# Low parts of the input projections' weights: a subtraction on VectorE, or a transfer that adds the weight to minus its high part

## The chip, the cores and the metric

The kernel runs on one core of a Trainium2 chip (trn2). The metric is the device time of one execution in microseconds (µs), as a median over runs. Five engines matter here, each with a queue of its own that it works through in order: PE (TensorE, matmuls), DVE (VectorE), ACT (ScalarE), POOL (GpSimd) and SP (SyncE, which here only issues DMA transfers). ACT and POOL issue transfers too. All transfers run on the core's 16 DMA engines.

## The reference

One decoder block on 512 tokens with 16 learned tokens ahead of them, 528 positions of width 1024:

```
h   = LN([meta; x])
p   = h @ W_in                      # 1024 -> 2048 (conformer) + 3360 (RWKV-7) + 2048 (two gates)
A   = proj(swish(LN(dwconv31(GLU(p_conv)))))
Bm  = proj(groupnorm(RWKV-7 recurrence over p_rwkv) * g)
h   = LN(alpha*h + (sigmoid(gA)*A + sigmoid(gB)*Bm) @ W_o)
out = LN(alpha*h + down(silu(u2)*u1)),   u = dwconv3(h @ ffn_up)
```

Everything is float32. The change concerns only how `W_in` is made ready for the matmuls of `p`.

## The kernel before, in words

**Two halves of each operand.** A matmul in the faster type float32r reads fewer bits than float32. So each operand is kept as a high part, rounded to float32r, and a low part, the rest. `gemm` (line 158) then adds up three products for each of the 8 slices of 128 input channels: high weight by high input (line 161), low weight by high input (162), high weight by low input (163). A weight tile of 128 output channels by 1024 input channels is 512 KB. It meets 528 columns in two halves of 272 and 256 (gates: 258 and 256), so one tile is worth 2 x 24 matmuls.

**Weights.** `wload` (line 155) and `wsplit` (143) make a tile ready: SP loads it into `wr` (two buffers), ACT rounds it into `wh` (line 138, in the helper `split`), DVE subtracts `wh` from `wr` into `wl` (line 141). `wh` and `wl` have two buffers each, so tile i can be written only once the matmuls of tile i-2 have read that buffer. There are 151 such tiles in the program. 59 are of `W_in`: 3 for the low-rank columns, and 56 in three functions: `rkv` (line 339, keys, values and receptances of a pair of heads, 24 tiles), `glu` (679, two tiles for each of 8 channel blocks, 16 tiles) and `gate` (730, 16 tiles).

**Order of the work.** `SCHEDULE` (line 47) lists the steps. For each of 8 pairs of heads: K is `rkv`; P is `prep` (decays, keys and the small products `Gt`); S is `solve` (a triangular system in 31 dependent steps on DVE, lines 521 and 523, with the taps of a depthwise convolution, lines 715 and 723, put between them); C is `merge` and `chain` (9 chunks of the recurrence, small matmuls at line 581); F is `finish`. G is `glu`, A is `gate`, N is the convolution's layer norm. The framework's scheduler then lays the instructions of each engine in one fixed queue by priority and its own estimate of when they can run. On PE the matmuls of the weight tiles stand between the small ones of `prep` and `chain`.

**POOL** has little work: memsets, a few small subtractions, and in each solve four small transfers for the first chunk of 16 positions: `dA` out (line 496), two of `L` in (507), `dT` out (539) and `Gt` in (556). The first of the 31 steps stand behind the arrival of `L` (line 527 reads it).

Of the kernel before, what the change touches and what calls it, by code (L numbers as in the profile page):

```python
# [11 lines left out]
F32 = mybir.dt.float32  # L12
F32R = mybir.dt.float32r
AF = mybir.ActivationFunctionType
ALU = mybir.AluOpType
# [3 lines left out]
P = 128  # L19
D = 1024  # L20
NK = D // P
# [17 lines left out]
C_GA = C_LORA + 288  # L39
# [15 lines left out]
def hybrid_block(ctx: ExitStack, tc: tile.TileContext, a, out, dbg=None):  # L55
    nc = tc.nc
    V, S, G, TE = nc.vector, nc.scalar, nc.gpsimd, nc.tensor
# [13 lines left out]
    def behind(ins, first, why):  # L71
        tc.add_manual_dep(ins.ins, first.ins.name, mybir.DependencyInfo(mybir.DependencyClass.NoSync,
                                                                mybir.DependencyReason.DATA), reason=why)
# [62 lines left out]
    def split(dst_hi, dst_lo, src, hi_engine="s"):  # L136
        if hi_engine == "s":
            S.copy(out=dst_hi, in_=src)  # L138
        else:
            V.tensor_copy(out=dst_hi, in_=src)  # L140
        V.tensor_tensor(out=dst_lo, in0=src, in1=dst_hi.bitcast(F32), op=ALU.subtract)  # L141

    def wsplit(raw_ap, shape, wpool, after=None, bufs=2):
        wpool = wpool or wp
        with nullcontext() if after is not None else front():
            raw = wp.tile(shape, F32, name="wr", tag="wr", bufs=2)
            load = nc.sync.dma_start(out=raw, in_=raw_ap)
            if after is not None:
                behind(load, after, "weights behind the input")
            hi = wpool.tile(shape, F32R, name="wh", tag="wh", bufs=bufs)  # L150
            lo = wpool.tile(shape, F32R, name="wl", tag="wl", bufs=bufs)
            split(hi, lo, raw)
        return hi, lo

    def wload(dram, c0, wpool=None, after=None, bufs=2):
        return wsplit(dram[:, c0:c0 + P].rearrange("(k p) n -> p k n", p=P), [P, NK, P], wpool, after, bufs)

    def gemm(ps, w, xh, xl, sl, nk=NK):
        wh, wl = w
# [8 lines left out]
    w_in = a["w_in"][0]  # L168
# [6 lines left out]
    def dcol(c, j=0, n=1):  # L175
        return drv[:, c + j:c + j + n]
# [28 lines left out]
    def shifted_gemm(dst, off, w, mi, rows=P):  # L205
        for hf in range(2):
            shifted_half(dst, off, w, mi, hf, rows)
# [15 lines left out]
    with tc.tile_pool(name="start", bufs=1, side="right", reuse_waits="tile") as st:  # L223
        prow = [st.tile([P, P], F32, name=f"prow{i}") for i in range(6)]
        with front():
            xt = []
            for i in range(5):
                n = NMETA if i == 0 else P
# [69 lines left out]
        c0 = 43  # L298
        for i, n in ((1, 112), (2, 128), (3, 120), (4, 88), (5, 44)):
# [15 lines left out]
                    in1=taps[:, :, 1, :], op=ALU.add)  # L315
# [23 lines left out]
    def rkv(p):  # L339
        k = ra.tile([P, OFF + T], F32, name="k", bufs=2)  # L340
        v = ra.tile([P, 64 + OFF + T], F32, name="v", bufs=2)
        r = ra.tile([P, OFF + T], F32, name="r", bufs=2)
        for i, (dst, c, off) in enumerate(((k, C_K, OFF), (v, C_V, OFF + 64), (r, C_R, OFF))):
            shifted_gemm(dst, off, wload(w_in, c + P * p), p + (8, 16, 0)[i])
        return r, k, v

    def prep(p, r, k, v):
# [329 lines left out]
    pair = lambda x: x.rearrange("p (m two) -> p two m", two=2)  # L677

    def glu(j):
        w2 = wload(w_in, 1024 + P * j)  # L680
        w1 = wload(w_in, P * j)
        cpad = ra.tile([P, 2, (KC - 1 + T) // 2], F32, name="cpad", bufs=3)
        G.memset(cpad[:, :, 0:KC // 2], 0.0)
        col2 = lambda t: (KC - 1 + t) // 2
        for t0, t1 in HALF:
            n = t1 - t0
            pt = gbank()
            gemm(pt[:, :n], w2, hh, hl, slice(t0, t1))
            with front():
                S.activation(out=cpad[:, :, col2(t0):col2(t1)], in_=pair(pt[:, :n]), func=AF.Tanh, scale=0.5)  # L690
        for t0, t1 in HALF:
            n = t1 - t0
            pt = gbank()
            gemm(pt[:, :n], w1, hh, hl, slice(t0, t1))
            with front():
                c_ = cpad[:, :, col2(t0):col2(t1)]
                V.scalar_tensor_tensor(out=c_, in0=c_, scalar=1.0, in1=pair(pt[:, :n]), op0=ALU.add, op1=ALU.mult)
        return cpad
# [28 lines left out]


    def gate(j):
        w = wload(w_in, C_GA + P * j)  # L730
        gt = sp.tile([P, NQ], F32, name="gt", bufs=2)
        for t0, t1 in QH:
            pt = gbank()
            n = t1 - t0
            gemm(pt[:, :n], w, hh, hl, slice(t0, t1))
            with front():
                S.activation(out=gt[:, t0 - Q0:t1 - Q0], in_=pt[:, :n], func=AF.Tanh, scale=0.5,
                             bias=dcol(D_HBG, j))
        nc.sync.dma_start(out=g_dr[j], in_=gt)
# [45 lines left out]
    raw, prs, solved, ys, cpads = {}, {}, {}, {}, {}  # L785
    gates = list(range(16))
    for step in SCHEDULE.split():
        what, p, q = step[0], int(step[1:2] or 0), int(step[2:] or -1)
# [23 lines left out]
    for j in range(NK):  # L812
        ga = rb.tile([P, NQ], F32, name="ga", bufs=2)
        nc.sync.dma_start(out=ga, in_=g_dr[j])
        w = wload(a["w_conv_out"][0], P * j)
# [12 lines left out]
    op = pool(ctx_o, "rout", "left")  # L828
# [10 lines left out]
    for j in range(NK):  # L839
# [4 lines left out]
        w = wload(a["w_rwkv_out"][0], P * j)  # L844
# [20 lines left out]
    for (t0, t1), (sl, n) in zip(QH, qsl):  # L865
# [3 lines left out]
        for j in range(NK):  # L869
            w = kept[j] if j < NKEEP else wload(a["w_o"][0], P * j)  # L870
# [3 lines left out]
            with front():  # L874
                V.scalar_tensor_tensor(out=x1, in0=hlo[:, j, t0:t1].bitcast(F32), scalar=ALPHA,
                                       in1=pt[:, :n], op0=ALU.mult, op1=ALU.add)
                V.scalar_tensor_tensor(out=x1, in0=hhi[:, j, t0:t1].bitcast(F32), scalar=ALPHA,
                                       in1=x1, op0=ALU.mult, op1=ALU.add)
# [57 lines left out]
    for j in range(2, NF):  # L936
        c = j - 2
# [80 lines left out]
```

## Time and profile before

| | |
|---|---|
| median of 3 runs | 1212.67 µs (1209.79 to 1213.87) |
| the profiled execution | 1205.18 µs, its span 1203.4 µs |
| PE busy | 1126.6 µs (94%) |
| DVE busy | 895.8 µs (74%) |
| ACT busy | 536.9 µs (45%) |
| POOL busy | 104.8 µs (9%) |
| moved by DMA | 119.00 MB |

A busy time is the union of an engine's instruction spans. Matmuls overlap, so a row of PE lasts longer (290 ns) than the distance to the next one (about 120 ns), and a busy PE need not be one at its peak. "Idle before, releaser" says how long an engine stood still ahead of an instruction and what ended that. The chain of waits is followed back from the last instruction to whatever released each piece of work.

### The profile page before, as it was taken

What the parts mean: (1) busy time and instruction counts of PE and PEld (TensorE: products, weight loads), DVE (VectorE), ACT (ScalarE), POOL (GpSimd) and SP (SyncE); (2) the same over time, 40 slices, a digit from 0 to 9 for tenths busy, and PEclk for the clock granted to TensorE, in tenths of its full rate; (3) what the DMA queues carried; (4) which work ended last, traced back from release to release, by engine and by line L of the source; (5) the groups of instructions that cost most, each with busy time, mean ns of one, the idle gap of its engine ahead of it and who ended that gap; (6) DMA issues with size and microseconds to landing.
All of it is one profiled execution on the core that took longest, in us unless ns stands there. A gap on an engine that the chain in (4) does not pass through costs nothing.

```text
span 1203.4 us, 22828 instructions
## 1 busy us (share of the span) xinstructions
PE 1126.6 (94%) x8718; PEld 1052.9 (87%) x8718; DVE 895.8 (74%) x2299; ACT 536.9 (45%) x1123; POOL 104.8 (9%) x250
## 2 busy tenths in 40 slices
PE   5999989899999979999886999999999999999997
PEld 3998979888898979999775989999999999998885
DVE  8599978988899898997487446688867666662227
ACT  3543445546455456565466333346443344431111
POOL 6001011201202021120200000000000000000000
PEclk9999999998999999999997999999999999999999
DMA  5233332333324233353541385622423233243221
GB/s 159 80 92 90 85 88 63 80 72 88 78 74 99 52 75 82 93 129 88 142 132 24 117 242 159 175 80 63 132 71 106 80 96 101 78 125 119 88 88 70
DMA packets 202440, 119.00 MB, mean 99 GB/s; under 512 B 50036, under 2 KB 186397, under 8 KB 202331
## 3 DMA queue, kind: packets, MB, share of 16 engines
q1 hardware_dynamic: 182992, 113.81, 33.4%
q10 hardware_dynamic: 17515, 3.17, 1.5%
q8 instruction: 68, 1.11, 0.4%
q0 software_dynamic: 1824, 0.57, 0.2%
q14 instruction: 41, 0.34, 0.1%
HBM read 102.24 MB, written 15.28 MB: 98 GB/s over the span
## 4 chain that ended last, share of the span: by engine, by line
PE 67%; DVE 18%; DMA 7%; issue 4%; ACT 4%; ACTq 0%; POOL 0%; DVEq 0%; SPq 0%; POOLq 0%
PE ps_g L161 16%; PE ps_g L163 15%; PE ps_g L162 15%; PE ps_x L581 8%; PE psf L962 3%; PE psf L964 3%; PE psf L963 3%; DVE wl L141 2%; DVE csh L715 2%; DVE cev L723 1%; DMA o_t<-o_dr 1%; DVE W L523 1%; DVE stmp L521 1%; DMA L<-dA 1%; DMA dA<-Gt 1%
## 5 line engine op out<-in xcount | busy, mean ns | idle before, releaser
L161 PE MATMUL ps_g<-hhi,wh 128*128 128x256 f32 (+2 forms) x1648 | 477.9, 290 | 14.0 <-ACT cpad L690 4.0
L163 PE MATMUL ps_g<-hlo,wh 128*128 128x256 f32 (+2 forms) x1648 | 475.6, 289 | 0.0
L162 PE MATMUL ps_g<-hhi,wl 128*128 128x256 f32 (+2 forms) x1648 | 475.5, 289 | 0.0
L161 PEld LDWEIGHTS ps_g<-hhi,wh 128*128 128x128 f32 x1648 | 313.0, 190 | 18.4 <-ACT hf_t L277 4.6
L163 PEld LDWEIGHTS ps_g<-hlo,wh 128*128 128x128 f32 x1648 | 313.0, 190 | 1.3
L162 PEld LDWEIGHTS ps_g<-hhi,wl 128*128 128x128 f32 x1648 | 312.2, 189 | 1.4 <-issue 0.4
L141 DVE TENSOR_TENSOR wl<-wr,wh 128x1024 fp32r<-128x1024 f32 x151 | 184.2, 1221 | 99.7 <-ACT wh L138 99.2
L138 ACT CAST wh<-wr 128x1024 fp32r<-128x1024 f32 x151 | 158.0, 1047 | 150.1 <-PE psf L963 75.2
L723 DVE SCALAR_TENSOR_TENSOR cev<-cd,drv,cev 128x257 f32<-128x257 f32 x216 | 98.2, 478 | 0.1
L920 ACT COPY pu<-ps_g 128x258 f32<-128x258 f32 (+1 forms) x88 | 32.9, 374 | 110.3 <-PE ps_g L163 110.2
L962 PE MATMUL psf<-wh,hidh 128*128 128x512 f32 x176 | 69.3, 394 | 0.0
L964 PE MATMUL psf<-wl,hidh 128*128 128x512 f32 x176 | 68.9, 391 | 0.0
L963 PE MATMUL psf<-wh,hidl 128*128 128x512 f32 x176 | 68.5, 389 | 0.0
L927 DVE SCALAR_TENSOR_TENSOR u<-pu,prm,u 128x512 f32<-128x512 f32 x88 | 65.7, 748 | 1.3
L581 PE MATMUL ps_x<-UV,Gt 128*66 128x64 f32 x576 | 59.2, 224 | 3.6 <-DMA Gt<-dT 1.7
L581 PEld LDWEIGHTS ps_x<-UV,Gt 128*66 128x66 f32 x576 | 53.5, 140 | 5.5 <-DVE on L673 2.3
L715 DVE SCALAR_TENSOR_TENSOR csh<-cpad,drv,csh 128x257 f32<-128x257 f32 x120 | 57.5, 479 | 0.4
L614 DVE SCALAR_TENSOR_TENSOR Sb<-Sb,lc,ps_x 64x64 f32<-64x64 f32 x112 | 31.3, 279 | 34.7 <-PE ps_x L581 33.1
L521 DVE TENSOR_TENSOR stmp<-L,W 128x60 f32<-128x60 f32 (+24 forms) x248 | 55.3, 223 | 1.1
L600 ACT COPY Rz<-ps_x 64x128 f32<-64x128 f32 x72 | 18.6, 259 | 82.6 <-PE ps_x L581 63.2
L523 DVE TENSOR_TENSOR W<-W,stmp 128x60 f32<-128x60 f32 (+24 forms) x248 | 53.3, 215 | 1.3
L925 DVE TENSOR_SCALAR u<-pu,prm 128x512 f32<-128x512 f32 x44 | 21.2, 484 | 43.1 <-ACT pu L920 43.0
(310 smaller groups left out, 2022.9 us busy)
## 6 DMA issues: line engine op xcount, KB each, us to landing
wr<-in_w_in_dram SPq DMA_DIRECT2D x59, 512.0 KB, 4.1
wr<-in_ffn_up_dram SPq DMA_DIRECT2D x44, 512.0 KB, 3.9
wr<-in_ffn_down_dram SPq DMA_DIRECT2D x22, 512.0 KB, 3.7
wr<-in_w_o_dram SPq DMA_DIRECT2D x10, 512.0 KB, 4.3
g_dr<-gt SPq DMA_DIRECT2D x16, 257.0 KB, 3.1
L<-dA SPq DMA_DIRECT2D x32, 128.0 KB, 3.8
wr<-in_w_conv_out_dram SPq DMA_DIRECT2D x8, 512.0 KB, 4.3
wr<-in_w_rwkv_out_dram SPq DMA_DIRECT2D x8, 512.0 KB, 5.3
```

The source lines that it names most:

```text
L138: S.copy(out=dst_hi, in_=src)
L141: V.tensor_tensor(out=dst_lo, in0=src, in1=dst_hi.bitcast(F32), op=ALU.subtract)
L161: TE.matmul(ps, wh[:, k, :], xh(k, sl), start=(k == 0), stop=False)
L162: TE.matmul(ps, wl[:, k, :], xh(k, sl), start=False, stop=False)
L163: TE.matmul(ps, wh[:, k, :], xl(k, sl), start=False, stop=(k == nk - 1))
L521: yield V.tensor_tensor(out=tv, in0=L[:, s, s + 1:32].unsqueeze(1).broadcast_to([P, nj, m]), in1=W[:, 0:nj, s:s + 1].broadcast_to([P, nj, ...
L581: mm = lambda o, l, r, start: TE.matmul(o, l, r, start=start, stop=True, skip_group_check=True)
L715: yield V.scalar_tensor_tensor(out=cs_, in0=x1[:, i:i + NM], scalar=dcol(D_SCW, 8 * i + j) if i < HT else dcol(D_HCW, 8 * 2 * i + j), in1= ...
L723: yield V.scalar_tensor_tensor(out=yp[:, b, :] if lasttap else ev[:, b, :], in0=d[:, i:i + NM], scalar=dcol(D_HCW, 8 * (2 * i + b) + j), i ...
L962: TE.matmul(acc[t][d], hidh[:, k, ts], wd[k][0][:, ds], start=(k == 0), stop=False)
L963: TE.matmul(acc[t][d], hidl[:, k, ts], wd[k][0][:, ds], start=False, stop=False)
L964: TE.matmul(acc[t][d], hidh[:, k, ts], wd[k][1][:, ds], start=False, stop=(k == NF - 1))
```

## The change

The functions that load weights get a parameter `add`, which `rkv`, `glu` and `gate` set. ACT still rounds the tile into `wh`. With `add`, ACT also writes minus the tile, rounded in the same way, into `wl`; then POOL issues a transfer that reads the 512 KB of the weight from DRAM a second time and adds it to what stands in `wl`. Without `add` the subtraction on DVE stays (95 tiles).

```diff
-    def wsplit(raw_ap, shape, wpool, after=None, bufs=2):
+
+    def wsplit(raw_ap, shape, wpool, after=None, bufs=2, add=False):
         wpool = wpool or wp
         with nullcontext() if after is not None else front():
             raw = wp.tile(shape, F32, name="wr", tag="wr", bufs=2)
             load = nc.sync.dma_start(out=raw, in_=raw_ap)
+            hi = wpool.tile(shape, F32R, name="wh", tag="wh", bufs=bufs)
+            lo = wpool.tile(shape, F32R, name="wl", tag="wl", bufs=bufs)
             if after is not None:
                 behind(load, after, "weights behind the input")
-            hi = wpool.tile(shape, F32R, name="wh", tag="wh", bufs=bufs)
-            lo = wpool.tile(shape, F32R, name="wl", tag="wl", bufs=bufs)
-            split(hi, lo, raw)
+            S.copy(out=hi, in_=raw)
+            if add:
+                S.mul(out=lo, in_=raw, mul=-1.0)
+                G.dma_start(out=lo, in_=raw_ap, accum_op=ALU.add)
+            else:
+                V.tensor_tensor(out=lo, in0=raw, in1=hi.bitcast(F32), op=ALU.subtract)
         return hi, lo
...
-            shifted_gemm(dst, off, wload(w_in, c + P * p), p + (8, 16, 0)[i])
+            shifted_gemm(dst, off, wload(w_in, c + P * p, add=True), p + (8, 16, 0)[i])
...
-        w2 = wload(w_in, 1024 + P * j)
-        w1 = wload(w_in, P * j)
+        w2 = wload(w_in, 1024 + P * j, add=True)
+        w1 = wload(w_in, P * j, add=True)
...
-        w = wload(w_in, C_GA + P * j)
+        w = wload(w_in, C_GA + P * j, add=True)
```

Lines behind this place carry numbers that are 6 higher after the change. The scheduler lays all queues anew.

The first place is ACT's queue at the three `W_in` tiles that are made ready while the first pair's `k`, `v` and `r` are projected (`k`, `v`, `r`: the projections that ACT and DVE take out of the PSUM bank `ps_g`, in halves of 272 and 255 columns). Before:

```order
L199 ACTIVATE k<-ps_g,prm 128x272
L199 ACTIVATE k<-ps_g,prm 128x255
L138 CAST wh<-wr 128x1024
L402 ACTIVATE sq<-k,prm 128x576
L199 ACTIVATE v<-ps_g,prm 128x272
L199 ACTIVATE v<-ps_g,prm 128x255
L138 CAST wh<-wr 128x1024
L199 ACTIVATE r<-ps_g,prm 128x272
L199 ACTIVATE r<-ps_g,prm 128x255
L138 CAST wh<-wr 128x1024
```

After:

```order
L205 ACTIVATE k<-ps_g,prm 128x272
L155 ACTIVATE wl<-wr 128x1024
L205 ACTIVATE k<-ps_g,prm 128x255
L153 CAST wh<-wr 128x1024
L408 ACTIVATE sq<-k,prm 128x576
L205 ACTIVATE v<-ps_g,prm 128x272
L155 ACTIVATE wl<-wr 128x1024
L205 ACTIVATE v<-ps_g,prm 128x255
L153 CAST wh<-wr 128x1024
L205 ACTIVATE r<-ps_g,prm 128x272
L155 ACTIVATE wl<-wr 128x1024
L205 ACTIVATE r<-ps_g,prm 128x255
```

The negation stands ahead of the second half of each projection, and the cast behind it.

The second place is POOL's queue around the second pair's solve (`dA`, `L`, `dT`: the small transfers of the solve). Before:

```order
L193 MEMSET r 128x49
L496 DMA dA_2233<-Gt 16x2x16
L507 DMA L_2245<-dA_2233 16x256 x2
L511 MEMSET W 128x256
L514 MEMSET W 32x8 x4
L458 TENSOR_TENSOR AR<-AR,lc 128x1024
L193 MEMSET v 128x113
L683 MEMSET cpad 128x2x15
L539 DMA dT_2235<-W_2246 32x16
L556 DMA Gt<-dT_2235 16x2x16
L515 COPY W_3280<-w_init 32x16
```

After:

```order
L156 DMA wl<-in_w_in_dram 128x8x128
L502 DMA dA_2248<-Gt 16x2x16
L513 DMA L_2260<-dA_2248 16x256 x2
L464 TENSOR_TENSOR AR<-AR,lc 128x1024
L156 DMA wl<-in_w_in_dram 128x8x128
L545 DMA dT_2250<-W_2261 32x16
L517 MEMSET W 128x256
L520 MEMSET W 32x8 x4
L199 MEMSET v 128x113
L562 DMA Gt<-dT_2250 16x2x16
L521 COPY W_3303<-w_init 32x16
L156 DMA wl<-in_w_in_dram 128x8x128 x3
```

An adding transfer now stands directly ahead of `dA` and one directly ahead of `dT`.

## Rows read from the trace of the kernel before

**Rows 1.** Busy time, share of the span, instructions; then stretch 50 to 600, DMA share last

```profile
PE 1126.6 (94%) x8718; PEld 1052.9 (87%) x8718; DVE 895.8 (74%) x2299; ACT 536.9 (45%) x1123; POOL 104.8 (9%) x250
50.00:600.00 550.00, 521.40 (x4294) 485.00 (x4294) 478.81 (x1519) 278.94 (x662) 81.51 (x173) 0.99 0.35 88
```

**Rows 2.** What PE waited for, 50 to 620: us in total, times, longest

```profile
PE ps_g L161 <- ACT cpad L690: 4.0, 1, 4.0
PE ps_g L161 <- DVE r L201: 3.7, 4, 1.4
PE ps_m L563 <- DVE t11n L558: 3.1, 2, 2.5
...
PE ps_x L581 <- DMA Gt<-dT: 1.7, 1, 1.7
PE ps_a L471 <- DVE Gt L453: 1.6, 2, 0.8
PE ps_x L581 <- DVE on L673: 1.5, 2, 1.1
PE ps_a L467 <- DVE Gt L453: 1.3, 1, 1.3
```

**Rows 3.** Chain of waits, 50 to 650, by line

```profile
by line: PE ps_x L581 13.6%; PE ps_g L161 11.5%; PE ps_g L163 11.0%; PE ps_g L162 10.9%; issue 6.2%; DVE wl L141 3.3%; DVE csh L715 3.0%; DVE cev L723 2.7%; DVE W L523 2.6%; DVE stmp L521 2.5%; DMA L<-dA 2.2%; DMA dA<-Gt 1.4%; DVE Gt L453 1
```

**Rows 4.** Costliest groups of the page: busy us, mean ns of one, idle before

```profile
L141 DVE TENSOR_TENSOR wl<-wr,wh 128x1024 fp32r<-128x1024 f32 x151 | 184.2, 1221 | 99.7 <-ACT wh L138 99.2
L138 ACT CAST wh<-wr 128x1024 fp32r<-128x1024 f32 x151 | 158.0, 1047 | 150.1 <-PE psf L963 75.2
```

**Rows 5.** DMA queue and issues, 50 to 600: KB each, us from issue to landing

```profile
q1 hardware_dynamic: 90073, 45.23, 31.4%
...
wr<-in_w_in_dram SPq DMA_DIRECT2D x52, 512.0 KB, 4.1
...
L<-dA POOLq DMA_DIRECT2D x16, 16.0 KB, 2.3
dA<-Gt POOLq DMA_DIRECT2D x8, 2.0 KB, 2.0
```

**Rows 6.** Timeline of POOL, 12 to 14: start, duration of transfers of 16 and 128 rows

```profile
12.82 0.52 POOL L243 DMA_DIRECT2D prow<-in_b_gate_dram  x1
13.33 0.58 POOL L245 DMA_DIRECT2D prow<-in_conv_dw_dram  x1
```

**Rows 7.** Timeline of PE, ACT, DVE at one tile of `glu`: start, duration

```profile
51.69 0.28 PE L163 MATMUL ps_g<-hlo,wh 128*128 128x256 f32 x1
...
52.00 0.39 ACT L690 ACTIVATE cpad<-ps_g 128x256 f32<-128x256 f32 x1 [1.85 <-PE ps_g L163]
52.28 1.04 ACT L138 CAST wh<-wr 128x1024 fp32r<-128x1024 f32 x1
...
53.36 1.23 DVE L141 TENSOR_TENSOR wl<-wr,wh 128x1024 fp32r<-128x1024 f32 x1 [3.55 <-ACT wh L138]
...
57.66 0.29 PE L161 MATMUL ps_g<-hhi,wh 128*128 128x272 f32 x1
```

**Rows 8.** Timeline of PE at the last of the 56 tiles: start, duration

```profile
603.58 0.36 PE L163 MATMUL ps_g<-hlo,wh 128*128 128x256 f32 x1
...
615.16 0.28 PE L161 MATMUL ps_g<-hhi,wh 128*128 128x258 f32 x1
```

**Rows 9.** Chain of waits at the second solve, 160 to 180: start, us, what

```profile
160.84 3.63 DMA dA<-Gt
...
165.04 0.44 POOL L L507
...
165.56 4.30 DMA L<-dA
169.88 0.22 DVE W L527
```

More of the change, by code (lines that the diff above doesn't have):

```diff
@@ L147, in wsplit, with wload @@
             load = nc.sync.dma_start(out=raw, in_=raw_ap)
+            hi = wpool.tile(shape, F32R, name="wh", tag="wh", bufs=bufs)
+            lo = wpool.tile(shape, F32R, name="wl", tag="wl", bufs=bufs)
             if after is not None:
                 behind(load, after, "weights behind the input")
-            hi = wpool.tile(shape, F32R, name="wh", tag="wh", bufs=bufs)
-            lo = wpool.tile(shape, F32R, name="wl", tag="wl", bufs=bufs)
-            split(hi, lo, raw)
+            S.copy(out=hi, in_=raw)
[4 more added lines that the diff above has]
+                V.tensor_tensor(out=lo, in0=raw, in1=hi.bitcast(F32), op=ALU.subtract)
         return hi, lo
-    def wload(dram, c0, wpool=None, after=None, bufs=2):
-        return wsplit(dram[:, c0:c0 + P].rearrange("(k p) n -> p k n", p=P), [P, NK, P], wpool, after, bufs)
+    def wload(dram, c0, wpool=None, after=None, bufs=2, add=False):
+        return wsplit(dram[:, c0:c0 + P].rearrange("(k p) n -> p k n", p=P), [P, NK, P], wpool, after, bufs, add)
     def gemm(ps, w, xh, xl, sl, nk=NK):
```

## The prediction, made before the changed kernel was run

> **What bounds the kernel now.** I read the busy times first. Over the span PE is busy 94%, and in the stretch from 50 to 600, in which nearly all of the 56 tiles are used, 521 of 550 µs, with DVE close behind at 479 (87%), ACT at 279 and POOL at 82 [rows 1]. So the question is whether DVE's 87% holds PE up. The list of PE's waits answers it: PE's visible waits on DVE in that stretch are few. The ones shown are 3.7 (a projection's evacuation), 3.1 (the merge), 1.6 and 1.3 (the small products) and 1.5 µs (`finish`) [rows 2], 11.2 µs together. The chain of waits says how far DVE stands behind PE where PE's own rows don't show it: the low-part subtraction, line 141, holds 3.3% of the chain from 50 to 650 [rows 3], 20 µs of 600. PE's own rows hold most of the chain. So this is a PE-bound stretch with DVE near the bound, and what DVE gets back is worth some 10 to 20 µs, not its whole busy time.
>
> **What goes.** 56 of 151 subtractions at 1.221 µs [rows 4] leave DVE, 68.4 µs of busy time. On the path they are worth between 0 (the next piece of DVE work, a tap of the convolution, takes the place) and 20 µs (all that the chain shows). I take 14: the 11.2 µs of waits shown and a little for those too short to be shown.
>
> **What comes, on ACT.** 56 negations of 128x1024. Nothing of that operation is in the trace; the nearest row is the cast of the same tile on the same engine, 1.047 µs [rows 4]. 56 x 1.047 = 59 µs, on an engine that is idle half of the stretch [rows 1]. As busy time I cost it at nothing. Its place costs something: in ACT's new queue the negation stands ahead of the second half of a projection's evacuation, which comes 1.05 µs later, and `r` of each pair feeds `prep`. Between 0 and 8 pairs x 1.05 = 8 µs; I take 3, since PE has other tiles to work on. Should PE have none left, it is the 8.
>
> **What comes, on POOL.** 56 transfers of 1024 runs of 512 bytes. POOL takes 0.52 µs to issue 16 rows and 0.58 for 128 [rows 6], 0.5 ns a row; 1024 rows would take about 1.0 µs by that line, an estimate. 56 µs on an engine that is busy 82 of 550 [rows 1]: hidden. Not hidden is the order. The queue is in order, the adding transfer waits for ACT, ACT's negation waits for PE to release the buffer, and now `dA` and `L` of a solve stand behind it. That pair of hops is on the chain already in the second solve: `dA` 3.63 µs, `L` 4.30 µs, then the first step of line 527 [rows 9]. The same small transfers land in 2.0 and 2.3 µs as a median [rows 5], so there was something ahead of them there. Behind an adding transfer each hop can lose its 2 µs of data: 0 to 8 pairs x 2 hops x 2 µs = 32 µs. I take 4, for a quarter of the hops and half of the 2 µs, because the second copy of the system, which comes through SP, has to arrive too.
>
> **The main term: when is `wl` ready.** Before, a tile whose buffer came free at 51.94 (0.25 µs after the start of the last matmul) had its cast at 52.28 and its subtraction done at 54.59, 2.7 µs after release; its first matmul came at 57.66 [rows 7]. So PE never waited for a low part there. I call the time from the last matmul of tile i-2 to the first of tile i the window: 57.66 - 51.94 = 5.7 µs here, 11.3 µs at the last of the 56 [rows 7, 8]. I measured all 56 in the same way: nine are 5.7 to 5.8 µs, ten lie from 6.1 to 7.7, and 37 from 8.7 to 20.4. After the change the window must hold the negation (1.05), the hand-over between engines (about 0.15) and the transfer from issue to landing, L.
>
> L is not in the trace. Bounds from the nearest rows: the plain load of the same 512 KB lands in 4.1 µs [rows 5]. Its packets took 31.4% of 16 engines over 550 µs for 90073 packets [rows 5], 30.7 ns each; 1024 packets on 16 engines are 2.0 µs of streaming, and the other 2.1 µs are latency, as the 2 KB transfer's 2.0 µs also say. An addition has to fetch what stands in `wl` as well. If that fetch costs nothing, L = 4.1; if it streams once more, L = 2.1 + 2 x 2.0 = 6.1; if reading back, adding and writing follow one another as two whole transfers, L = 8.2. I take 6.2, the middle, and keep both ends.
>
> Then I go through the 56 windows in order. A tile waits if 1.2 + L is longer than its window, and the wait lengthens the next window by as much, so in a run of short ones only every second pays. With L = 4.1 (5.3 µs) no window is too short. With L = 6.2 (7.4 µs) 12 tiles wait, **15 µs** together. With L = 8.2 (9.4 µs) 17 tiles wait, **41 µs**. The windows are those of the old PE queue; the new one breaks up some of the dense runs and makes others.
>
> The Trainium skill has a rule against this change. Its page "Collectives: The Full Stack", section "The bandwidth ceiling: the fold count and why AG ≠ RS ≠ AR", says that an addition inside a transfer is slow not for its arithmetic but because it needs two source reads, which halves the rate. No run here shows it yet. By it L would be the 6.1 and the sum mine; by the plain load's row the 15 µs would be nothing and the sum about 7 µs faster than before.
>
> **Sum.** -14 (DVE) + 15 (PE waits for `wl`) + 3 (evacuation) + 4 (solve's small transfers) = +8 µs on the profiled execution's 1205.18, which is 7.5 below the median of 1212.67. I carry the difference over to the median: **1221 µs**. A measurement of this kernel tells about 0.3% (3.6 µs) from no change.
>
> **Rivals.**
> 1. *Faster: the transfer lands like a plain load.* With L below about 4.5 no window is too short, and the whole of DVE's relief shows. For it: POOL's small transfers land in 2.0 µs, which is just the latency of the plain load [rows 5], and 37 of 56 windows have 3 µs to spare even at L = 4.3. Against it: the destination has to be read. Price: -20 (the subtraction's part of the chain [rows 3], with the costs of order hidden behind DVE's gain), so 1193. The skill's page "DMA: Bandwidth & Descriptors", section "Anatomy of one DMA — SWDGE (gpsimd) path", has a fit for transfers issued from GpSimd, 2.0 µs plus bytes over 436 KB per µs. For 512 KB that gives an estimate of 3.2 µs, under the 4.1 that this trace shows for a load through SP; it would put the time here.
> 2. *Much slower: the addition is slow or POOL's issue is.* With L = 8.2 the waits are 41 µs: -14 + 41 + 3 + 4 = +34, 1247; every further µs of L costs some 16 µs (17 to 24 tiles wait, most of them for all of it), so L = 9.5 gives about 1268. For it: a read and a write of the same bytes in one transfer, 1024 short runs, a conversion to float32r. Against it: POOL's issue time hardly grows with the rows [rows 6].
> 3. *It does nothing that can be seen:* DVE's relief is taken by the next tap, the windows of the new queue are long enough, 1213. The new queues show 56 transfers and 95 subtractions, so the change does say what it does.
>
> **Chances.** The forecast 0.44 (of that faster 0.06, same 0.11, slower 0.27; its own range 1208 to 1236), rival 1 0.33 (faster 0.29, same 0.04), rival 2 0.20 (slower), rival 3 0.03 (faster 0.01, same 0.01, slower 0.01). Together faster 0.36, same 0.16, slower 0.48. The range goes from 1184, rival 1 with another 9 µs from stalls too short for the list, to 1268, rival 2 at L = 9.5; what is left out is a slower addition still, or solves that lose the full 32 µs, and a larger gain.
>
> **What would show it.** Right: DVE 68 µs less busy, ACT 59 more, the adding transfer landing in 5.5 to 7 µs, and new waits of PE on it at line 168 (low weight) of some 15 µs, in 10 to 15 places, with the waits on DVE mostly gone. Wrong to the fast side: landing under 4.5 µs and no such waits. Wrong to the slow side: landing over 8 µs, or POOL busy for several µs at each issue, or long waits of line 527 for `L`. If the transfer lands as I say and the time still falls, my 14 µs for DVE was too little: then PE's hidden stalls between rows depend on DVE more than its waits show.

## The result, and the profile after

1278.96 µs as a median (1276.71 to 1287.9), against 1211.23 µs (1206.77 to 1213.87) of the kernel before on the same chip: slower by 5.8%, ratio 1.0577, 95% interval 1.0516 to 1.0638. That is 58 µs above the forecast and 11 µs above the upper end of the range. The profiled execution took 1278.51 µs, its span 1276.8.

The page of the changed kernel, busy times, granted clock, queues, groups and transfers:

```profile
PE 1153.7 (90%) x8718; PEld 1081.0 (85%) x8718; DVE 843.4 (66%) x2243; ACT 588.6 (46%) x1179; POOL 190.9 (15%) x306
...
PEclk9889899999998899999887799999999999999999
...
q0 software_dynamic: 60064, 29.93, 19.0%
...
L168 PE MATMUL ps_g<-hhi,wl 128*128 128x256 f32 (+2 forms) x1648 | 491.2, 298 | 68.1 <-DMA wl<-in_w_in_dram 68.1
...
L158 DVE TENSOR_TENSOR wl<-wr,wh 128x1024 fp32r<-128x1024 f32 x95 | 115.9, 1222 | 86.4 <-ACT wh L153 86.2
L156 POOL DMA_DIRECT2D wl<-in_w_in_dram x56 | 88.4, 1579 | 261.4 <-ACT wl L155 171.1
...
L155 ACT ACTIVATE wl<-wr 128x1024 fp32r<-128x1024 f32 x56 | 59.3, 1058 | 45.5 <-PE ps_g L168 40.1
...
wr<-in_w_in_dram SPq DMA_DIRECT2D x59, 512.0 KB, 5.2
wl<-in_w_in_dram POOLq DMA_DIRECT2D x56, 512.0 KB, 8.7
```

The 56 subtractions are gone: 95 of 151 are left, and their group falls from 184.2 µs [rows 4] to 115.9. DVE's busy time falls by 52 µs only [rows 1], since it is a union of spans and these overlap. The negation costs ACT 1.058 µs each, and the adding transfer lands in 8.7 µs. Issuing it takes POOL 1.58 µs. The stretch 50 to 600 and its queues, to be read against [rows 1, 5]:

```profile
50.00:600.00 550.00, 485.81 (x3800) 451.68 (x3801) 399.97 (x1354) 291.24 (x632) 146.55 (x215) 0.94 0.69 118
```

```profile
q0 software_dynamic: 49992, 24.92, 37.0%
q1 hardware_dynamic: 77482, 37.41, 29.6%
...
wl<-in_w_in_dram POOLq DMA_DIRECT2D x47, 512.0 KB, 8.6
wr<-in_w_in_dram SPq DMA_DIRECT2D x46, 512.0 KB, 5.4
...
L<-dA POOLq DMA_DIRECT2D x14, 16.0 KB, 2.1
dA<-Gt POOLq DMA_DIRECT2D x7, 2.0 KB, 3.2
```

PE got through 3800 matmuls instead of 4294, its mean granted clock fell from 0.99 to 0.94, and the DMA engines are busy for 0.69 of the time instead of 0.35. The plain load of the same tile slowed from 4.1 to 5.4 µs. PE's waits from 50 to 620, against [rows 2]:

```profile
PE ps_g L168 <- DMA wl<-in_w_in_dram: 55.3, 21, 6.8
PE ps_m L569 <- DVE t11n L564: 5.7, 3, 3.6
PE ps_a L477 <- DVE Gt L459: 1.5, 1, 1.5
```

The chain of waits from 50 to 700, by line, against [rows 3]:

```profile
by line: DMA wl<-in_w_in_dram 6.3%; issue 2.0%; PE ps_g L168 1.8%; PE ps_g L169 1.6%; PE ps_x L587 1.5%; PE ps_g L167 1.5%; DMA dA<-Gt 1.2%; DMA dB<-Gt 1.1%; DVE W L533 0.6%; DMA a21s<-dB 0.5%; DVE cev L729 0.5%; DMA L<-dA 0.3%; DVE Gt L459
```

The subtraction, 3.3% before, is not among the entries shown; the transfer is the largest. (The rows name only part of this chain's time, so only their order is used.)

One tile in the timeline, against [rows 7]; columns are start, duration. The tile whose low part is late here is `r` of the first pair, and its buffer was last read by the matmuls of `k`. In [rows 7] too the tile that is made ready is one of `rkv`, `k`; only the tile that frees the buffer is one of `glu`.

```profile
77.42 1.06 ACT L155 ACTIVATE wl<-wr 128x1024 fp32r<-128x1024 f32 x1 [2.23 <-PE ps_g L168]
...
78.78 1.55 POOL L156 DMA_DIRECT2D wl<-in_w_in_dram  x1 [10.83 <-ACT wl L155]
...
83.20 0.29 PE L167 MATMUL ps_g<-hhi,wh 128*128 128x272 f32 x1
...
87.20 0.47 PE L168 MATMUL ps_g<-hhi,wl 128*128 128x272 f32 x1 [3.71 <-DMA wl<-in_w_in_dram]
...
87.47 0.43 PE L169 MATMUL ps_g<-hlo,wh 128*128 128x272 f32 x1
...
87.70 0.43 PE L167 MATMUL ps_g<-hhi,wh 128*128 128x272 f32 x1
```

The window is the 5.7 µs of [rows 7]: the buffer is free at about 77.4 and PE asks for the tile at 83.2. Negation and hand-over take 1.4 µs and the transfer 8.4 µs, so PE does one matmul and stands still for 3.7 µs. Behind the wait the matmuls start 0.23 µs apart instead of 0.12. The same place in stretches of 5 µs (PE, PEld, DVE, ACT, POOL, then granted clock, DMA share and GB/s):

```profile
75.00:80.00 5.00, 5.00 (x44) 5.00 (x43) 4.50 (x10) 2.73 (x5) 1.22 (x1) 1.00 0.01 3
80.00:85.00 5.00, 3.48 (x30) 3.27 (x28) 4.86 (x12) 2.78 (x5) 0.82 (x3) 1.00 0.86 152
85.00:90.00 5.00, 2.80 (x13) 2.80 (x14) 2.47 (x7) 0.63 (x1) 1.18 (x1) 0.74 1.08 175
90.00:95.00 5.00, 5.00 (x40) 5.00 (x40) 2.50 (x7) 0.89 (x2) 0.00 (x0) 0.92 0.69 92
```

After the stall PE runs at the lower of its two clock levels (1.2 instead of 2.4 GHz) until about 90.6. So this wait costs twice: once as idle time, once as slower matmuls, and the list of waits shows only the first.

### The profile page after: what moved, and what is told of

It reads as the page before. It is cut to its first block, busy times and chain, and to the rows that moved or that the text cites. A ratio compares the mean times of both kernels' runs of the same rounds, so it can differ in the third digit from the quotient of the medians.

```text
span 1276.8 us, 22884 instructions
## 1 busy us (share of the span) xinstructions
PE 1153.7 (90%) x8718; PEld 1081.0 (85%) x8718; DVE 843.4 (66%) x2243; ACT 588.6 (46%) x1179; POOL 190.9 (15%) x306
## 3 DMA queue, kind: packets, MB, share of 16 engines
q0 software_dynamic: 60064, 29.93, 19.0%
## 4 chain that ended last, share of the span: by engine, by line
PE 37%; DMA 9%; DVE 5%; issue 2%; ACT 2%; POOL 0%; SPq 0%; DVEq 0%; ACTq 0%; POOLq 0%
PE ps_g L168 9%; PE ps_g L167 9%; PE ps_g L169 9%; DMA wl<-in_w_in_dram 3%; PE psf L968 3%; PE psf L970 3%; PE psf L969 3%; PE ps_x L587 2%; DMA wr<-in_w_o_dram 2%; DMA o_t<-o_dr 1%; ACT wh L153 1%; DMA wr<-in_ffn_up_dram 1%; DMA dA<-Gt 1%; DVE wl L158 1%; DMA dB<-Gt 1%
## 5 line engine op out<-in xcount | busy, mean ns | idle before, releaser
L168 PE MATMUL ps_g<-hhi,wl 128*128 128x256 f32 (+2 forms) x1648 | 491.2, 298 | 68.1 <-DMA wl<-in_w_in_dram 68.1
L167 PE MATMUL ps_g<-hhi,wh 128*128 128x256 f32 (+2 forms) x1648 | 488.0, 297 | 6.1 <-ACT hf_t L283 4.3
L169 PE MATMUL ps_g<-hlo,wh 128*128 128x256 f32 (+2 forms) x1648 | 486.6, 296 | 0.0
L168 PEld LDWEIGHTS ps_g<-hhi,wl 128*128 128x128 f32 x1648 | 324.6, 197 | 74.9 <-DMA wl<-in_w_in_dram 73.2
L167 PEld LDWEIGHTS ps_g<-hhi,wh 128*128 128x128 f32 x1648 | 324.8, 197 | 8.0 <-ACT hf_t L283 5.0
L169 PEld LDWEIGHTS ps_g<-hlo,wh 128*128 128x128 f32 x1648 | 325.1, 197 | 1.6 <-issue 0.2
L158 DVE TENSOR_TENSOR wl<-wr,wh 128x1024 fp32r<-128x1024 f32 x95 | 115.9, 1222 | 86.4 <-ACT wh L153 86.2
L156 POOL DMA_DIRECT2D wl<-in_w_in_dram x56 | 88.4, 1579 | 261.4 <-ACT wl L155 171.1
L155 ACT ACTIVATE wl<-wr 128x1024 fp32r<-128x1024 f32 x56 | 59.3, 1058 | 45.5 <-PE ps_g L168 40.1
```

The costliest lines, as they stand in the source:

```text
L156: G.dma_start(out=lo, in_=raw_ap, accum_op=ALU.add)
L158: V.tensor_tensor(out=lo, in0=raw, in1=hi.bitcast(F32), op=ALU.subtract)
L167: TE.matmul(ps, wh[:, k, :], xh(k, sl), start=(k == 0), stop=False)
L168: TE.matmul(ps, wl[:, k, :], xh(k, sl), start=False, stop=False)
L169: TE.matmul(ps, wh[:, k, :], xl(k, sl), start=False, stop=(k == nk - 1))
```

## The experiments

The accounts of all kernels, from their profiled executions. "Other idle" is the span less PE's busy time less its waits for `wl`. The times are medians, each ratio is to the kernel before timed beside that run (medians of 1208.1 to 1211.2 µs), and one execution can lie 7 µs from its median (e5 was profiled at 1211.7, e8 at 1195.3). Every edit also makes the scheduler lay all queues anew; how much of a small difference between two kernels is that alone was not measured.

| kernel | time, µs | ratio to before | PE busy | waits for `wl` | other idle | clock |
|---|---|---|---|---|---|---|
| before | 1211.2 | 1 | 1126.6 | 0 | 76.8 | 0.981 |
| the change | 1279.0 | 1.0577 | 1153.7 | 68.1 | 55.0 | 0.954 |
| e1 no transfer | 1179.2 | 0.9748 | 1121.2 | 0 | 58.2 | 0.984 |
| e2 no addition | 1217.7 | 1.0071 | 1129.5 | 25.1 | 57.3 | 0.977 |
| e3 low part in the middle | 1226.4 | 1.0143 | 1133.4 | 2.4 | 84.0 | 0.970 |
| e8 as e3, no transfer | 1187.9 | 0.9846 | 1126.3 | 0 | 67.3 | 0.978 |
| e4 POOL subtracts | 1265.8 | 1.0470 | 1151.2 | 2.4 | 113.4 | 0.961 |
| e5 source in SBUF | 1219.2 | 1.0079 | 1134.4 | 12.4 | 63.2 | 0.973 |
| e12 as e5, short pieces | 1257.9 | 1.0414 | 1151.2 | 32.4 | 71.2 | 0.957 |
| e9 = e3 + e5 | 1216.7 | 1.0077 | 1133.5 | 0.5 | 77.8 | 0.971 |
| e13 small ones on ACT | 1279.7 | 1.0594 | 1152.2 | 62.9 | 60.9 | 0.958 |
| e19 three tiny transfers | 1268.0 | 1.0473 | 1156.3 | 55.7 | 59.3 | 0.955 |
| e6 gates only | 1246.5 | 1.0324 | 1143.5 | 14.9 | 80.1 | 0.964 |
| e16 `glu` only | 1246.5 | 1.0312 | 1149.4 | 17.1 | 78.2 | 0.957 |
| e15 `glu` only, SBUF | 1211.1 | 1.0020 | 1134.8 | 4.5 | 68.6 | 0.971 |
| e11 `rkv` only, SBUF | 1226.8 | 1.0137 | 1137.2 | 11.6 | 76.0 | 0.970 |
| e10 no gates, SBUF | 1206.0 | 0.9987 | 1133.1 | 14.0 | 61.7 | 0.975 |
| e17 as e10, in halves | 1218.6 | 1.0082 | 1133.9 | 3.6 | 77.8 | 0.975 |
| e18 as e10, low part last | 1200.2 | 0.9929 | 1127.3 | 4.8 | 67.0 | 0.981 |

### What DVE's relief is worth: e1

```diff
-                G.dma_start(out=lo, in_=raw_ap, accum_op=ALU.add)
```

> Leaves out the adding transfers of the 56 tiles, so their low part is minus the high part and those products are not the reference's. Theory A (the loss is the transfer landing later than the two buffers allow): without it no wait of PE for a low part is left, DVE still has its 68 us back, and the kernel falls below the one before, to 1190 to 1208 us. Rival B (the loss is the newly laid order of the queues, with the negations ahead of evacuations): most of the 68 us stay, over 1240 us. Rival C (DVE's relief is worth nothing on the path): 1208 to 1222 us.

Measured: 1179.17 µs, ratio 0.9748 (0.9712 to 0.9784), 31 µs faster than before, with the negations on ACT in it, and below even theory A's 1190 to 1208. So the change has a large gain in it, and the transfer costs 100 µs. The spans say how: from e1's 1179.4 to the change's 1276.8 are 97.4 µs, which are 68.1 of waits for `wl`, 32.5 more of PE's busy time and 3.2 less of other idle time. e1's page:

```profile
PE 1121.2 (95%) x8718; PEld 1051.7 (89%) x8718; DVE 848.4 (72%) x2243; ACT 586.7 (50%) x1179; POOL 105.9 (9%) x250
```

Where the relief shows, in stretches of before and then of e1 (columns as above):

```profile
450.00:550.00 100.00, 97.46 (x817) 90.53 (x817) 90.25 (x298) 58.21 (x142) 17.21 (x30) 0.98 0.39 101
550.00:650.00 100.00, 82.56 (x635) 73.05 (x634) 73.76 (x244) 59.22 (x136) 9.13 (x18) 0.88 0.37 101
650.00:750.00 100.00, 94.29 (x766) 89.72 (x766) 49.82 (x110) 39.20 (x79) 0.00 (x0) 0.98 0.55 160
```

```profile
450.00:550.00 100.00, 97.41 (x834) 90.05 (x833) 79.77 (x304) 66.67 (x149) 10.01 (x22) 1.00 0.36 93
550.00:650.00 100.00, 87.09 (x684) 78.97 (x682) 66.66 (x204) 61.94 (x143) 7.02 (x15) 0.88 0.39 103
650.00:750.00 100.00, 99.99 (x832) 98.73 (x831) 58.48 (x113) 37.99 (x64) 0.00 (x0) 1.00 0.67 198
```

Added up over rows of 100 µs, of which the last is shown, e1 issued 4005 matmuls from 50 to 550 and before 3910, 95 ahead; from 550 to 750 it gained another 115. At some 0.125 µs a matmul that is 12 µs and 14 µs. The second half lies behind the stretch that the prediction read. In before, one slice of it is DVE's alone:

```profile
620.00:640.00 20.00, 11.18 (x50) 7.94 (x48) 19.29 (x58) 15.70 (x34) 1.69 (x2) 0.65 0.23 73
```

There the convolution's layer norm and the last solves fill DVE (19.29 of 20 µs), and PE is at 11.18 with a granted clock of 0.65. The largest of all of PE's waits before is for `zh`, the output of that norm; e1's list no longer has it:

```profile
PE ps_g L161 <- ACT zh L138: 8.0, 2, 7.1
```

That it is DVE's relief which brings the gain there is read from these rows; no run parts it from the newly laid order.

### What the transfer's time is made of: e2, e5, e12

e2 takes the addition away, e5 reads the tile that already lies in SBUF, and e12 does that in pieces of 512 bytes again (a gap of 4 elements after each slice of the destination).

```diff
-                G.dma_start(out=lo, in_=raw_ap, accum_op=ALU.add)
+                G.dma_start(out=lo, in_=raw_ap)                     # e2
+                G.dma_start(out=lo, in_=raw, accum_op=ALU.add)      # e5, e12
...
-            lo = wpool.tile(shape, F32R, name="wl", tag="wl", bufs=bufs)
+            lo = wpool.tile([P, NK, P + 4], F32R, name="wl", tag="wl", bufs=bufs)[:, :, 0:P]   # e12, with add
```

> The same transfers from POOL without the addition: they load the weight over the negation, so the low part is the whole weight and those products are not the reference's. If the addition's second read is what makes the transfer late, it lands in 4.1 to 5.5 us, POOL issues it in about 1.0 us, and the kernel takes 1195 to 1220 us. If POOL's way of issuing 1024 runs is what costs, the landing stays at 7.5 us or more, the issue at 1.5 us, and the time over 1255 us.

> The adding transfer reads the tile that the load has already brought into SBUF (`raw`, 4 KB in a row per partition) instead of the weight in DRAM (1024 runs of 512 bytes). Theory 1, the number of short pieces sets both issue (1.57 us) and landing (8.7 us): issue falls to 0.6 to 0.7 us, landing to about 6 us, PE's waits for the transferred tile to 10 to 20 us, and the time to about 1215 to 1230. Theory 2, the addition itself (fetch, add, write) sets the landing: issue may fall, landing stays at 8 to 9 us, and the time stays within 1265 to 1280. Under both, the tile in SBUF is released later, so the load of the tile after next can be late by some us, which neither counts.

> As e5, but the low part's tile has a gap of 16 bytes after each 512, so that the adding transfer between two SBUF tiles again consists of 1024 pieces of 512 bytes, as in the change, but without the second read from DRAM. Theory 1, the pieces set the price: issue back at 1.5 to 1.6 us, landing at 7.5 to 9 us and the time at 1260 to 1285, as the change. Theory 2, the read from DRAM sets it: issue 0.9 us, landing 5 to 5.5 us, 1215 to 1225, as e5. Half and half, if issue rises and landing hardly: 1225 to 1250.

Measured: 1217.73 µs (ratio 1.0071, 1.0044 to 1.0098), 1219.17 (1.0079, 1.0054 to 1.0105) and 1257.94 (1.0414, 1.0364 to 1.0465). The pages of e2, e5 and e12, POOL's group and the transfers:

```profile
q0 software_dynamic: 60064, 29.93, 15.5%
...
L156 POOL DMA_DIRECT2D wl<-in_w_in_dram x56 | 50.4, 901 | 251.7 <-ACT wl L155 176.3
...
wl<-in_w_in_dram POOLq DMA_DIRECT2D x56, 512.0 KB, 5.8
```

```profile
q0 software_dynamic: 9888, 29.93, 13.1%
...
L156 POOL DMA_DIRECT2D wl<-wr x56 | 49.3, 880 | 232.9 <-ACT wl L155 174.4
...
wl<-wr POOLq DMA_DIRECT2D x56, 512.0 KB, 5.1
```

```profile
q0 software_dynamic: 60064, 29.93, 20.7%
...
L156 POOL DMA_DIRECT2D wl<-wr x56 | 88.1, 1574 | 237.7 <-ACT wl L155 148.5
...
wl<-wr POOLq DMA_DIRECT2D x56, 512.0 KB, 6.6
```

With the same bytes, landing goes from 5.1 µs (long pieces in SBUF) to 6.6 (short pieces in SBUF) to 8.7 (short pieces from DRAM), and without the addition to 5.8. The time follows: 1219, 1258, 1279. So 39 of the 60 µs between e5 and the change go with the short pieces and 21 with the second read from DRAM. e2 comes near its first case (it lands at 5.8 where 4.1 to 5.5 was expected), e5 is its theory 1 with a longer issue than the 0.6 to 0.7 expected. e12 lies between its theories: the issue is wholly back, the landing and the time only in part. Neither alone makes the issue long: it is 0.90 µs for short pieces without addition, 0.88 for long ones with it, and 1.57 only for short pieces with addition.

### Waits or traffic: e13, e14, e19

e13 issues the solve's four small transfers from ACT's queue. e14 sends the adding transfer into a scratch tile in DRAM. e19 puts three dependent transfers of 2 KB in its place.

```diff
-        G.dma_start(out=dA0.rearrange("h s t -> s h t"), in_=Gt[OFF:64, :, 0, OFF:64])
+        nc.scalar.dma_start(out=dA0.rearrange("h s t -> s h t"), in_=Gt[OFF:64, :, 0, OFF:64])   # e13; L0, dT0, Gt likewise
...
-                G.dma_start(out=lo, in_=raw_ap, accum_op=ALU.add)
+                G.dma_start(out=dr.tile(shape, F32, name="ws", tag="ws", bufs=4), in_=raw_ap, accum_op=ALU.add)   # e14
+                for _ in range(3):                                                                                # e19
+                    G.dma_start(out=lo[0:16, 0, 0:32], in_=raw_ap[0:16, 0, 0:32], accum_op=ALU.add)
```

> The changed kernel with the solve's small transfers (dA, L, dT, Gt of the first chunk) issued from ACT's queue instead of POOL's, so that none stands behind an adding transfer any more. Theory 1, as predicted, their place in POOL's queue costs little: 4 us, so 1272 to 1282. Theory 2, the small transfers in POOL's queue are much of what is left when the waits for the transferred tile are taken away (e3's and e9's +38 and +29 over e8): 1240 to 1262.

> The changed kernel, but the adding transfer goes into a scratch tile in DRAM that nobody reads; the low part stays minus the high part. All traffic (512 KB read in pieces of 512 bytes, added, written) and POOL's issues are there, and no engine waits for the transfer. Theory 1, the rest of the price beyond TensorE's waits (after less its 68 us of waits is 1211, e3 and e9 stand 38 and 29 us over e8) is the transfers' getting in the way of loads and of the solve's small transfers: 1195 to 1215. Theory 2, the rest is what follows from the waits themselves (the half clock after a stall, the order of the pairs that slips): 1177 to 1187, as e1.

> Each adding transfer is replaced by three of 2 KB each that follow one another (each adds to the same corner of the low part's tile), so that the tile is ready about as late as in the change, 6 to 8 us after the negation, with hardly any bytes on the DMA engines. The low part is otherwise left at minus the high part. Theory 1, the price is the wait and the slower clock after it: waits for the tile of 30 to 70 us, TensorE's busy time 15 to 35 us over e1's 1121 in step with them, and a time of 1225 to 1275. Theory 2, it takes the traffic to slow TensorE: waits as said, but TensorE's busy time stays at 1121 to 1128, so 1210 to 1245 at most, e1 plus the waits.

e13: 1279.65 µs (1.0594, 1.0542 to 1.0646), the change's own time, so theory 1: the place in POOL's queue costs nothing measurable over a place in ACT's queue. e14: 1340.94 µs (1.1096, 1.1069 to 1.1122) and no answer, for with nobody waiting the scheduler put all 56 transfers at the head of POOL's queue, ahead of the constants that PE needs:

```profile
PE ps_m L259 <- POOL ident masks.py:199: 163.7, 1, 163.7
```

e19: 1267.96 µs (1.0473, 1.0437 to 1.0508). Its page and PE's waits:

```profile
PE 1156.3 (91%) x8718; PEld 1079.3 (85%) x8718; DVE 847.1 (67%) x2243; ACT 589.3 (46%) x1180; POOL 230.4 (18%) x418
...
q0 software_dynamic: 7200, 0.92, 0.8%
```

```profile
PE ps_g L169 <- DMA wl<-in_w_in_dram: 55.7, 24, 5.9
```

With 0.92 MB instead of 29.93 in that queue PE waits 55.7 µs and is busy 35.1 µs longer than in e1. Theory 1 holds: waiting alone gives both parts of the price, and no traffic is needed. What the traffic does besides is lengthen the landing.

### Longer windows: e3, e8, e9

```diff
+        if low is not None:     # first half of a tile: its low products last; second half: first
+            seq = [(h, k) for k in range(nk) for h in (0, 2)]
+            lows = [(1, k) for k in range(nk)]
+            seq = lows + seq if low else seq + lows
...
```

e8 is this order without the transfer, e9 this order with e5's source.

> The adding transfers stay; only the order of a tile's 48 matmuls changes: the 16 that read the low part stand together in the middle (last in the first half, first in the second), so its buffer comes free 16 matmuls earlier and is needed 16 later, and each window grows by 2 x 16 x 0.12 = 3.8 us. Theory A: with 8.7 us to land and 1.2 us ahead of it, windows of 9.5 us and more are nearly enough; PE's waits for the low part fall from 68 to under 15 us, the time to 1195 to 1222 us. Rival B (order of the queues, DMA traffic and the solve's small transfers behind the adding ones): the waits move elsewhere and the time stays over 1245 us.

> The order of e3 (the low part's matmuls of a tile together in the middle) without the adding transfer: the low part is left at minus the high part. This is the control for e3 (1226) and e1 (1179). Theory 1, the order of the matmuls costs nothing: the time is e1's, 1176 to 1184, and all of e3's +47 us is the transfer, though TensorE no longer waits for its tile. Theory 2, the order itself costs (low-part buffers are released later in the tile, high-part ones too): 1195 to 1220, and the transfer's remaining price is only the rest up to 1226.

> e3's order and e5's source together: a right result, no second read from DRAM, and windows that are 3.8 us longer. Theory 1, what is left of e3's price is bytes and pieces on the DMA engines: with 128 long pieces per tile instead of 1024 short ones the loads and the solve's small transfers are held up less, and the time falls from 1226 to 1190 to 1210, under the kernel before. Theory 2, what is left is the addition's time on the DMA engines or the order itself: 1220 to 1230, as e3.

Measured: 1226.44 µs (1.0143, 1.0112 to 1.0173), 1187.93 (0.9846, 0.9811 to 0.9881) and 1216.73 (1.0077, 1.0050 to 1.0105). All three lie between their two theories. Against the change e3 gets back 52 µs, by taking away 66 of the 68 µs of waits; the same transfer, landing in 7.3 µs, is then hidden from the tile's own matmuls. The order costs 9 µs by itself (e8 less e1), less than theory 2 had it. Yet e3 and e9 stay 38 and 29 µs over e8 with almost no wait for `wl`. In the profiled executions, where e8 ran 7 µs over its median, other idle time is 17 and 11 µs higher and PE's busy time 7, and the spans differ by only 26 and 18 µs. Which of the many smaller waits makes that up isn't settled; e13 speaks against the place of the small transfers in POOL's queue.

### Which tiles: e6, e16, e15, e11, e10

Only the calls with `add=True` differ: e6 and e16 keep the change's transfer for the gates and for `glu` alone; e15, e11 and e10 use e5's source for `glu`, for `rkv`, and for both.

> Only the 16 tiles of the gates are made by the adding transfer; the other 40 keep the subtraction on VectorE. Theory 1, each tile costs where its window is short: the time lies by the number of gate tiles with a wait; with 16 of 56 tiles and the +69 us spread evenly over them 1230; if the gates stand in the long windows, their waits are under 5 us, VectorE gives back 16 of 56 of the 31 us that e1 showed, 9 us, and the time is 1200 to 1207. Theory 2, the transfers cost mostly by getting in the way of other transfers (those of the solve and the loads): 16 of 56 of e3's +47 over e1, 13 us, less the 9, so 1210 to 1218.

> Only the 16 tiles of `glu`, with the change's own transfer from DRAM (512-byte pieces, landing at 8.7 us). The windows of `glu`'s second tiles are 5.7 us, so by the landing each of 8 waits some 4 us. Theory 1: 15 to 30 us over e15. Theory 2, within 8 us of e15: with few transfers the landing is hidden by the queue's other work.

> Only the 16 tiles of `glu` are made by the transfer (from the tile in SBUF, as e5). Theory 1, the three groups add up: e5 less e10 makes the gates cost 12, e11 makes keys, values and receptances cost 17 to 18, so `glu` alone gives 18 to 20 us: 1186 to 1194, faster than both kernels, because its tiles stand beside the taps of the convolution, where VectorE is fullest. Theory 2, they don't add up (one schedule differs from another by as much): 1200 to 1215.

> As e10, and the 16 tiles of `glu` back on VectorE as well: 24 tiles, those of keys, values and receptances, are made by the transfer. Theory 1: what counts is the number of transfers in the way of the solve's small ones; with 24 instead of 40 the time lies between the kernel before and e10. Theory 2: the tiles of `glu`, whose windows were 5.7 us, carry the remaining waits, and without them PE's waits for the transferred tile are under 3 us and the time is the best of the three, 1190 to 1203.

> As e5 (the tile in SBUF as source), but the 16 gate tiles keep the subtraction on VectorE; 40 tiles are made by the transfer. e6 showed that from 520 to 640 us, where the gate tiles stand close together, VectorE is busy under half of the time, so the transfer takes nothing off a busy engine there. Theory 1, a transfer pays only where VectorE is full: the gates' share of e5's +10 goes and the gain of the rest stays, 1198 to 1208, at or just under the kernel before. Theory 2, the transfers of the other 40 tiles cost as much as they give too: 1208 to 1220, no better than e5.

Measured: 1246.46 µs (1.0324, 1.0292 to 1.0355), 1246.46 (1.0312, 1.0292 to 1.0333), 1211.06 (1.0020, 1.0001 to 1.0038), 1226.77 (1.0137, 1.0080 to 1.0195) and 1206.04 (0.9987, 0.9962 to 1.0012). These expectations were mostly wrong: the groups do not add up. 16 tiles with the change's own transfer cost 37 to 38 µs, in either of the two groups, where all 56 cost 68. The table hints at why: with 16 or 24 tiles the other idle time stays near before's 76.8 µs (68.6 to 80.1), with 40 or 56 it falls to 55 to 63 in the change, e2, e5 and e10. That the relief comes only once much of DVE's work is gone is a reading of these rows and not shown: e12 with 56 tiles has 71.2 and e17 with 40 has 77.8. e15 at 1211 is its theory 2, that the groups don't add up, and not the 1186 to 1194 of the sum.

### A version that is faster: e17, e18, and POOL instead of the transfer: e4

e17 cuts e10's negation and transfer into two halves; e18 gives e10 a new order in the first half of each tile only, low part last; e4 lets POOL subtract.

```diff
+                for h in (slice(0, 4), slice(4, 8)):                                           # e17
+                    S.mul(out=lo[:, h, :], in_=raw[:, h, :], mul=-1.0)
+                    G.dma_start(out=lo[:, h, :], in_=raw[:, h, :], accum_op=ALU.add)
...
+        if low == 0:                                                                           # e18
+            seq = [(h, k) for k in range(nk) for h in (0, 2)] + [(1, k) for k in range(nk)]
...
+                G.tensor_tensor(out=lo, in0=raw, in1=hi.bitcast(F32), op=ALU.subtract)         # e4
```

> As e10 (glu, keys, values and receptances from the tile in SBUF), but negation and transfer each in two halves of 4 slices, so that the first low-part matmul waits for 256 KB only. Theory 1, what e10 (1206) lacks to e1's gain is its 14 us of waits and the slower matmuls behind them: the first half lands about 1 us earlier, the waits fall to 5 to 9 us, and the time to 1196 to 1203, under both kernels. Theory 2, twice the issues on POOL (80 x 0.6 to 0.9 us) and more transfers undo it: 1204 to 1215.

> As e10, but in the first half of each tile the 8 low-part matmuls come last, about 1.9 us later than before; the second half keeps its order. Theory 1: nearly all of e10's 14 us of waits go (its longest is 3.1 us), and the time falls to 1192 to 1202, under both kernels. Theory 2: the order costs as it did in e8 over e1 (9 us), and the time stays at 1203 to 1212.

> The 56 subtractions go to POOL as an instruction of its own in place of negation and transfer. The nearest row is a product of two operands of 128x1024 on POOL, 2.02 us. Theory A: a tile is then ready about 1.05 + 2.0 + 0.6 = 3.7 us after its buffer comes free, under the shortest window of 5.7, so no wait for low parts, and DVE has its 68 us back: 1190 to 1208 us. Rival C (DVE's relief worth nothing): 1208 to 1222. Rival D (POOL and DVE hold each other up when both read two operands): POOL's instruction takes over 3 us, DVE's get longer, 1215 us or more.

e17: 1218.56 µs (1.0082, 1.0051 to 1.0113): the waits for `wl` fall to 3.6 µs, and other idle time rises by as much as that saves and more, so that it is slower than even theory 2 had it. e18: 1200.16 µs (0.9929, 0.9902 to 0.9955), as theory 1 had it, **faster than both kernels**, 9 µs or 0.7% under before; waits 4.8 µs and PE's clock back at before's 0.981:

```profile
PE 1127.3 (94%) x8718; PEld 1054.3 (88%) x8718; DVE 862.3 (72%) x2259; ACT 573.2 (48%) x1163; POOL 139.1 (12%) x290
```

The kernel before with e18's order alone was not tried, so how much of the 9 µs belongs to the order is open.

e4: 1265.81 µs (1.0470, 1.0442 to 1.0499), rival D in the main. Each subtraction takes POOL 2.6 µs in the mean, not over 3, and DVE's own instructions grow longer beside it. Groups of e1, then of e4:

```profile
L526 DVE TENSOR_TENSOR stmp<-L,W 128x60 f32<-128x60 f32 (+24 forms) x248 | 53.1, 214 | 3.1
```

```profile
L526 DVE TENSOR_TENSOR stmp<-L,W 128x60 f32<-128x60 f32 (+24 forms) x248 | 83.0, 335 | 3.1 <-DMA L<-dA 0.3
```

DVE is busy for 943.0 µs, more than in the kernel before that did 56 subtractions more.

## Why the prediction was wrong

**The mechanism was right, the sign in part by luck.** PE got new waits on `wl` at line 168, and they outweigh DVE's relief. Two terms of the sum were mis-sized, and one was missing. With the relief that e1 shows (24 µs in spans, the negations included) the prediction's own +15 and +4 would have added up to -5, a faster kernel: the two mis-sized terms pulled opposite ways.

- **L, the failed step.** "I take 6.2, the middle": it measured 8.7 µs, above even the 8.2 of two whole transfers one after the other. The bound was built from the SP load's 4.1 µs [rows 5], but a transfer from POOL with the same 1024 pieces and no addition takes 5.8 (e2). The 30.7 ns a packet came from SP's queue; by the queues' shares (worked out under the rivals) POOL's plain packets held an engine for 50 ns and the adding ones for 65, so that 1024 of them are an estimated 3.2 and 4.1 µs of streaming instead of 2.0. The addition also made the issue 1.58 µs instead of the "about 1.0" drawn through two small transfers [rows 6]. The second read from DRAM slowed the loads of `wr` as well, with the addition or without (5.2 µs here, 5.7 in e2, 4.1 in e5). By the prediction's own scale, 16 µs for each further µs from 1247 at 8.2, 8.7 would have given 1255. The rest of the way to 1279 is in the next two points.
- **The walk through the windows** would give 49 µs for 8.7 (41 at 8.2 and 16 for each further µs) in 17 to 24 tiles; 68.1 µs in 24 places were measured. The count was near, the sum 19 short. Landings of up to 13.1 µs, for all of which a median stood, and the windows of the new queue, which were not measured, are possible reasons.
- **The missing term: the clock after a stall.** PE's busy time rose by 32.5 µs over e1. The prediction priced a wait at its length. e19 shows that waits bring this along; over the table PE's busy time goes with the granted clock (1121 at 0.984, 1134 at 0.973, 1151 at 0.957), though not with the length of the waits alone: e16 has 17 µs of waits and a clock of 0.957, e2 25 µs and 0.977. It goes better with all of PE's idle time, the waits for `wl` and the other idle together: the kernels with 58 to 88 µs of it have PE busy for 1121 to 1137 µs, those with 95 to 124 µs for 1144 to 1156, e4 with hardly a wait for `wl` among them.
- **DVE, "I take 14".** e1 gives 31 µs in medians and 24 in spans. The waits on DVE that were added up hardly went away: over the whole span PE waited 22.9 µs on DVE before and 21.5 in e1, while its waits on ACT fell from 34.4 to 16.8. About half of the gain (12 µs) came before 550; the rest came from 550 to 750, where DVE was full in slices and PE half idle, and the prediction had stopped reading at 620 (at 650 for the chain [rows 3] that gave the bound of 20).
- **ACT's negation (+3) and the small transfers (+4).** e1 contains the first and is faster by 31 µs all the same, so its own price stays unknown; e13 finds nothing for the second.

In sum, from before's span of 1203.4: -24.0 (e1) + 68.1 (waits for `wl`) + 32.5 (slower matmuls) - 3.2 (other idle) = +73.4, the change's 1276.8. The prediction had -14 + 3, + 15, nothing, and + 4.

**The rivals.** Rival 2 was what happened, with a higher price than it had. Rival 1 needed L under 4.5; even plain and from POOL it was 5.8. The fit of the Trainium skill for such transfers ("DMA: Bandwidth & Descriptors", section "Anatomy of one DMA — SWDGE (gpsimd) path"), which gave an estimate of 3.2, doesn't hold here, where the plain transfer took 5.8 beside the kernel's other traffic. The rule on the addition's two reads (the Trainium skill, "Collectives: The Full Stack", section "The bandwidth ceiling: the fold count and why AG ≠ RS ≠ AR"), which the page states for a collective's rings, points the right way, but the rate isn't halved: by the queue's shares a packet of the change held an engine for 65 ns (19.0% x 1276.8 x 16 / 60064) and one of e2 for 50 (15.5% x 1211.9 x 16 / 60064), 1.3 times as long.

## What to carry to other kernels

A transfer that takes the place of an engine's work is judged by its time from issue to landing against the shortest window of its buffer, and a stall of PE can cost, besides its length, a stretch at the lower clock behind it. Build such a transfer from few long pieces, from a copy already in SBUF where there is one, and let the consumer use what it has first (e18). And what an engine's relief is worth is read over the whole program: the slice where that engine is full and PE half idle may lie behind the stretch in which the changed work stands.

## What the hardware showed that was not expected

- POOL's issue time of an adding transfer depends on pieces and addition together: 0.88 µs with 144 packets a tile and addition (e5), 0.90 with 1040 and none (e2), 1.57 with 1040 and addition (e12). (A tile's packets are q0's total less the 1824 of before, over 56.)
- A subtraction on POOL and DVE's instructions hold each other up: POOL's took 2.3 to 6.0 µs, and the solve's products on DVE grew from 214 to 335 ns. The Trainium skill, "SBUF — State Buffer", section "Who interferes with whom", says that a DVE instruction with two inputs in SBUF contends with a GpSimd instruction that reads SBUF; the row agrees, since `L` and `W` both lie there.
- This one is the scheduler's doing and not the chip's: the adding transfers that nobody waits for moved to the head of their queue and held up the start by 164 µs (e14). An order that a dependence no longer holds can't be taken for granted.
